# The next stage's input, normalised and transposed tile by tile during the running product

## The chip, the cores and the metric

The kernel runs on one core of a Trainium2 chip. The metric is the device time of one execution in microseconds. The core has TensorE (matmuls, transposes), VectorE, ScalarE, GpSimd and SyncE, which here issues the DMAs. In the profile they are called PE (PEld is its weight load), DVE, ACT, POOL and SP.

## The reference

It computes two transformer-like blocks on 512 tokens of width 1024, in float32. What matters here is the chain of stages at the end of the first block and the start of the second:

```python
x = x + gate1 * (merged @ w_o[l])                              # product 1: out_proj
h2 = rms_norm(x, norm2_w[l]) * (1.0 + scale2) + shift2
ff = jnp.square(jax.nn.relu(h2 @ w_mlp1[l])) @ w_mlp2[l]       # product 2: w_mlp2
x = x + gate2 * ff
...
h = rms_norm_2(x, norm_g)                                      # rglru_layer
u = h @ w_in
...                                                            # convolution, gates, linear scan
x = x + y @ w_out                                              # product 3: w_out_a
h = rms_norm_2(x_stream, norm_kv)                              # mla_shared_kv, mla_layer
ckr = h @ w_dkv
```

Each of the three marked products ends in x, whose rows are normalised (one root mean square per token) and are the input of the next product.

## The kernel before

*Tiles.* x lies in SBUF with tokens on the partitions: four token tiles t = 0 to 3 of 128 tokens, each in two halves b of 512 columns. A product that ends in x (`gemm_tm`) runs block b = 0 and then b = 1; a block needs all four token tiles and all its weights, 128 rows of the contraction per matmul. Every float32 operand is split into a high and a low part, so each step is three matmuls (`mm3`, L168 to L170): high with high, high with low, low with high. A weight piece (`weight`, L153 to L159) is loaded into wr, cast to wh by ScalarE, and the difference wl is made by VectorE or GpSimd; each of wr, wh and wl has four buffers.

*The end of a product.* In the last block (`touter`) the order is token tile by token tile: all steps of t = 0, then of t = 1, and so on. After the last matmul of a tile, `resid` multiplies by the gate (rt, L920) and adds to x (L921; L923 where there is no gate) on VectorE. `half_stats` takes the squares on ScalarE (sqj, L293) and, in the last block, the root r on GpSimd (L298, L299).

*The start of the next stage.* `transpose_norm` comes after the product in the code. For each token tile and each half kg it makes xn = x times r (L267, on GpSimd; in the third case on VectorE for kg = 1), four TensorE transposes into PSUM (pt, L271), where needed a scale and shift (nh, L280 on ScalarE, L283 and L286 on VectorE), and the split into high (ScalarE, L163) and low (VectorE, L164). So there are 8 transposes per token tile and 32 per hand-over. The new product then starts: `gemm_cm` with `halves=4` works four output blocks on token columns 0 to 255, then the same four on 256 to 511.

*The three hand-overs* are: first, out_proj to mlp (h2, called h in the profile); second, the last chunk of w_mlp2 to rglru (ha); third, w_out_a to mla_in (hb). w_out_a has five weight pieces per block, the others four.

*What sets the order.* The code issues instructions in its own order, and the tile framework's scheduler may move one ahead of another where nothing forbids it. What comes out is a fixed queue per engine, and each engine works through its queue in order. A tile in a pool has to wait for earlier tiles on the same memory. Pools belong to a `phase`, opened and closed like a stack on the left or right side of SBUF: in the kernel before, those of the next stage (the buffers of xn, h2 and nh) are opened after the running product's are closed, and so may lie over them.

Of the kernel before, what the change touches and what calls it, by code (L numbers as in the profile page):

```python
# [52 lines left out]
PAD = [0, 16, 56, 0, 32, 0, 32, 0, 0, 0, 56, 0, 48, 32, 0, 0, 0, 0, 0, 0]  # L53
# [6 lines left out]
class Build:  # L60
# [14 lines left out]
    def phase(self, nt=0, nbig=0, side="left", nw=0, nf=0, nx=0, nq=0):  # L75

        i = self.nm("p")
        with ExitStack() as st:
# [3 lines left out]
            p = {"sm": pool("sm", 2), "c": pool("c", 1)}  # L82
# [6 lines left out]
            if nbig:  # L89
                p["big"] = pool("big", nbig)  # L90
# [5 lines left out]
            if PAD[self.np]:  # L96
                self.nc.gpsimd.memset(p["c"].tile([128, PAD[self.np]], F32, name="pad" + i, tag="pad"), 0.0)
# [103 lines left out]
    def gemm_tm(self, blocks, lhs, evac, n, touter=False, gain=None, group=NT):  # L201


        for b, blk in enumerate(blocks):
# [4 lines left out]
            for ap in blk:  # L209
# [4 lines left out]
            order = [(t, i) for t in range(NT) for i in range(len(blk))] if hold else \  # L214
                [(t, i) for t0 in range(0, NT, group) for i in range(len(blk)) for t in range(t0, t0 + group)]
            for t, i in order:
                if i == 0 and t >= group:
# [6 lines left out]
                if i == len(blk) - 1:  # L224
                    evac(b, t, pss[t][:, :n])

# [33 lines left out]
    def transpose_norm(self, xt, rs, hi, lo, g=None, sh=None, key="xa"):  # L260

        nc = self.nc
        for t in range(NT):
            x = xt(t)
            for kg in range(2):
# [21 lines left out]
                self.split(hi[d], lo[d], h)  # L287

# [673 lines left out]
    def rglru(self):  # L962
# [10 lines left out]
        lam = self.load("lru_lambda", [128, 10])  # L973
        for b in (br, bi):
            nc.vector.tensor_scalar(out=b, in0=b, scalar1=0.5, scalar2=None, op0=ALU.mult)
        sp = self.c([128, 10], "sp")
        nc.vector.tensor_scalar(out=lam, in0=lam, scalar1=-1.0, scalar2=None, op0=ALU.mult)
        self.softplus(sp, lam, [self.small([128, 10], "spt", bufs=3) for _ in range(3)])
        spp = self.c([128, 10], "spp")
        spn = self.c([128, 10], "spn")  # L980
        nc.vector.tensor_scalar(out=spp, in0=sp, scalar1=4.0, scalar2=None, op0=ALU.mult)
        nc.vector.tensor_scalar(out=spn, in0=sp, scalar1=-4.0, scalar2=None, op0=ALU.mult)
# [4 lines left out]
        def xin(i, ps):  # L987
            xbs[i] = self.taps(ps, cw[:, i], cb[:, i:i + 1], [-3, -2, -1, 0])
# [7 lines left out]
        def product(jobs, halves=0):  # L996
            self.gemm_cm([[a["w_in_a"][i + 10 * (f is gin)]] for f, i in jobs], rhs,
                         lambda m, ps: jobs[m][0](jobs[m][1], ps), halves=halves)

        product([(xin, 0), (xin, 1), (gin, 0), (gin, 1)], halves=4)  # L1000
        for i0 in range(0, 10, 5):
# [32 lines left out]
            for j in range(5):  # L1034
# [3 lines left out]
                with self.fills():  # L1038
# [24 lines left out]
    def mla_in(self):  # L1063
# [13 lines left out]
        hh, hl = self.big("hb", F32R), self.big("hb", F32R)  # L1077
        self.transpose_norm(lambda t: xv[:, t], self.r4, hh, hl, key="xb")
# [4 lines left out]
                     lambda b, t, ps: nc.scalar.copy(out=ck[:, t], in_=ps), 320, gain=nkv)  # L1083
# [192 lines left out]
def emit(tc, a, out, dbg=None, stages=("b1", "b2")):  # L1276
    with ExitStack() as ctx:
        b = Build(tc, ctx, a, out, dbg)
        tail = ctx.enter_context(ExitStack())
# [181 lines left out]
```

## Time and profile before

| | |
|---|---|
| time, median of 3 runs | 1675.04 us (1671.86 to 1677.4) |
| time of the profiled execution | 1674.92 us |
| its span, first to last instruction | 1673.1 us |
| mean granted TensorE clock | 0.986 of full |
| TensorE busy | 1591.9 us, 95% |
| VectorE, ScalarE, GpSimd busy | 1130.0, 784.3, 447.4 us |
| chain that ended last | TensorE 40%, VectorE 4%, ScalarE 2%, GpSimd 2%, issue 1% |
| all 96 transposes of the hand-overs wait for xn | 29.5 us of weight-load and matmul waits |

The profile is of one execution. An engine's busy share is a mean over stages; a wait is put down to what ended it last. In a timeline row, equal instructions that follow each other are merged (x4), the first number is the start, the second the length from the first start to the last end, and a wait before it stands in brackets with its releaser. Matmuls overlap: the distance between starts is what each costs.

### The profile page before, as it was taken

What the parts mean: (1) busy time and instruction counts of PE and PEld (TensorE: products, weight loads), DVE (VectorE), ACT (ScalarE), POOL (GpSimd) and SP (SyncE); (2) the same over time, 40 slices, a digit from 0 to 9 for tenths busy, and PEclk for the clock granted to TensorE, in tenths of its full rate; (3) what the DMA queues carried; (4) which work ended last, traced back from release to release, by engine and by line L of the source; (5) the groups of instructions that cost most, each with busy time, mean ns of one, the idle gap of its engine ahead of it and who ended that gap; (6) DMA issues with size and microseconds to landing.
All of it is one profiled execution on the core that took longest, in us unless ns stands there. A gap on an engine that the chain in (4) does not pass through costs nothing. (4 is left out here: it accounts for less than half of the span.)

```text
span 1673.1 us, 20895 instructions
## 1 busy us (share of the span) xinstructions
PE 1591.9 (95%) x7696; PEld 1287.8 (77%) x7696; DVE 1130.0 (68%) x1948; ACT 784.3 (47%) x1511; POOL 447.4 (27%) x329
## 2 busy tenths in 40 slices
PE   5989999999999999999989999999989899999998
PEld 3767677677678778778879888888878777888886
DVE  7899689789869888973463343434457865757883
ACT  4357446354456666662353232323336562455552
POOL 3314345244353334321042020201131101521012
PEclk9999999999999999999999999999999999999999
DMA  7511223234223122225322233333313221322211
GB/s 257 187 53 62 63 76 127 63 101 134 78 63 101 57 83 88 87 74 177 93 76 88 89 101 100 91 99 101 101 52 114 78 79 52 100 78 67 67 64 51
DMA packets 50648, 153.54 MB, mean 92 GB/s; under 512 B 8177, under 2 KB 12913, under 8 KB 50546
## 3 DMA queue, kind: packets, MB, share of 16 engines
q1 hardware_dynamic: 50546, 152.22, 28.4%
q8 instruction: 60, 0.98, 0.2%
q14 instruction: 42, 0.34, 0.1%
HBM read 150.10 MB, written 2.10 MB: 91 GB/s over the span
## 5 line engine op out<-in xcount | busy, mean ns | idle before, releaser
L156 ACT CAST wh<-wr 128x1024 fp32r<-128x1024 f32 (+5 forms) x245 | 239.9, 980 | 417.7 <-PE pm L169 185.4
L159 DVE TENSOR_TENSOR wl<-wr,wh 128x1024 fp32r<-128x1024 f32 (+2 forms) x170 | 200.0, 1178 | 216.0 <-ACT wh L156 215.6
L159 POOL TENSOR_TENSOR wl<-wr,wh 128x1024 fp32r<-128x1024 f32 (+3 forms) x75 | 175.6, 2341 | 552.8 <-ACT wh L156 512.0
L168 PE MATMUL pm<-hh,wh 128*128 128x512 f32 x432 | 174.0, 407 | 8.5 <-ACT hh L163 6.8
L169 PE MATMUL pm<-hl,wh 128*128 128x512 f32 x432 | 175.5, 406 | 3.9 <-POOL hl L164 3.8
L170 PE MATMUL pm<-hh,wl 128*128 128x512 f32 x432 | 172.6, 400 | 0.0
L950 POOL TENSOR_TENSOR r<-r 128x512 f32<-128x512 f32 x32 | 50.8, 1589 | 260.1 <-ACT r L949 260.1
L168 PE MATMUL pm<-h,wh 128*128 128x512 f32 (+1 forms) x288 | 105.5, 368 | 0.0
L169 PE MATMUL pm<-h,wh 128*128 128x512 f32 (+1 forms) x288 | 105.4, 366 | 0.0
L170 PE MATMUL pm<-h,wl 128*128 128x512 f32 (+1 forms) x288 | 105.3, 366 | 0.0
L168 PEld LDWEIGHTS pm<-hh,wh 128*128 128x128 f32 x432 | 81.9, 190 | 30.2 <-ACT hh L163 8.3
L169 PEld LDWEIGHTS pm<-hl,wh 128*128 128x128 f32 x432 | 82.2, 190 | 26.9 <-POOL hl L164 7.2
L170 PE MATMUL pm<-wh,rl 128*128 128x512 f32 x256 | 99.6, 389 | 0.0
L168 PE MATMUL pm<-wh,rh 128*128 128x512 f32 x256 | 99.6, 389 | 0.0
L169 PE MATMUL pm<-wl,rh 128*128 128x512 f32 x256 | 99.6, 389 | 0.0
L731 POOL TENSOR_SCALAR pr<-pr,psum 128x512 f32<-128x512 f32 x64 | 64.6, 1021 | 128.8 <-DVE psum L727 70.7
L170 PEld LDWEIGHTS pm<-hh,wl 128*128 128x128 f32 x432 | 82.2, 190 | 19.7 <-issue 3.1
L478 DVE SCALAR_TENSOR_TENSOR acc<-pm,conv_w_s,acc 128x510 f32<-128x510 f32 (+2 forms) x118 | 87.7, 743 | 12.9 <-ACT acc L469 11.9
L614 POOL TENSOR_TENSOR e<-e,w 128x512 f32<-128x512 f32 x32 | 52.0, 1626 | 100.3 <-ACT e L613 85.9
L257 DVE SCALAR_TENSOR_TENSOR wada<-wada,cs 128x1024 f32<-128x1024 f32 x48 | 68.2, 1431 | 15.5 <-DMA wada<-in_w_ada 15.1
L726 ACT ACTIVATE pr<-px,nmax 128x512 f32<-128x512 f32 (+2 forms) x96 | 60.4, 637 | 29.9 <-DVE nmax L723 24.0
L168 PE MATMUL pm<-ha,wh 128*128 128x512 f32 (+1 forms) x192 | 69.0, 362 | 4.8 <-DVE acc L478 4.8
(401 smaller groups left out, 4138.3 us busy)
## 6 DMA issues: line engine op xcount, KB each, us to landing
wr<-in_w_mlp SPq DMA_DIRECT2D x64, 512.0 KB, 3.5
wada<-in_w_ada SPq DMA_DIRECT2D x48, 512.0 KB, 4.0
wr<-in_w_xbc SPq DMA_DIRECT2D x24, 512.0 KB, 3.5
wr<-in_w_in_a SPq DMA_DIRECT2D x20, 512.0 KB, 3.5
wr<-in_w_z SPq DMA_DIRECT2D x16, 512.0 KB, 3.6
wr<-in_w_ssd_out SPq DMA_DIRECT2D x16, 512.0 KB, 3.5
wr<-in_w_gate SPq DMA_DIRECT2D x16, 512.0 KB, 3.8
wr<-in_w_qkv SPq DMA_DIRECT2D x16, 384.0 KB, 3.0
```

The costliest lines, as they stand in the source:

```text
L156: nc.scalar.copy(out=hi[:, :n], in_=raw[:, :n])
L159: eng.tensor_tensor(out=lo[:, :n], in0=raw[:, :n], in1=r32(hi[:, :n]), op=ALU.subtract)
L168: m(out, lhsT=lh, rhs=rh, start=start, stop=False)
L169: m(out, lhsT=lh, rhs=rl, start=False, stop=False)
L170: m(out, lhsT=ll, rhs=rh, start=False, stop=stop)
L257: nc.vector.scalar_tensor_tensor(out=w, in0=w, scalar=1.0, in1=self.cs, op0=ALU.mult, op1=ALU.mult, accum_out=self.modc[:, j:j + 1])
L478: nc.vector.scalar_tensor_tensor(out=acc[:, lo:hi], in0=ps[:, lo + o:hi + o], scalar=w[:, j:j + 1], in1=acc[:, lo:hi], op0=ALU.mult, op1=A ...
L614: self.e("ew").tensor_tensor(out=e, in0=e, in1=w, op=ALU.mult)
L726: nc.scalar.activation(out=e[:, :n], in_=p, func=AF.Exp, bias=nmax, accum_out=s)
L731: self.e("norm").tensor_scalar(out=e[:, :n], in0=e[:, :n], scalar1=s, scalar2=1.0, op0=ALU.mult, op1=ALU.mult)
L950: self.e("sq").tensor_tensor(out=r, in0=r, in1=r, op=ALU.mult)
```

## The change

The new stage's norm is cut into a function per token tile (`token_norm`), and its pools are opened before the running product, on the other side of SBUF or in place of closed ones. `gemm_tm` gets `pre`: before token tile t of the last block it norms, transposes and splits tile t - 2 (`trail`), and after the last tile, tile 2. Tile 3 is done inside the next product: in `gemm_cm` after three of the four blocks on the first half of the tokens (`mid`), in `gemm_tm` of w_dkv before the last weight (`late`), whose token tile 3 comes last of all. In the last block of w_out_a the first two of five weights now pass over all token tiles first. The constants of rglru are loaded later, norm_kv and norm_b earlier. Pads are allocated without a memset.

```diff
-            p = {"sm": pool("sm", 2), "c": pool("c", 1)}
+            p = {}
+            if bare:
+                p["big"] = pool("big", nbig)
+            if not bare:
+                p["sm"] = pool("sm", 2)
+            if bare is not True:
+                p["c"] = pool("c", 1)
...
-                self.nc.gpsimd.memset(p["c"].tile([128, PAD[self.np]], F32, name="pad" + i, tag="pad"), 0.0)
+                p["c"].tile([128, PAD[self.np]], F32, name="pad" + i, tag="pad")
...
-    def gemm_cm(self, blocks, rhs, evac, halves=0, kouter=0, gain=None):
+    def gemm_cm(self, blocks, rhs, evac, halves=0, kouter=0, gain=None, mid=None):
...
+                        if mid and m == 0 and c0 == 0 and i == n - 2:
+                            mid()
...
-    def gemm_tm(self, blocks, lhs, evac, n, touter=False, gain=None, group=NT):
+    def gemm_tm(self, blocks, lhs, evac, n, touter=False, gain=None, group=NT, pre=None,
+                late=None):
...
-            order = [(t, i) for t in range(NT) for i in range(len(blk))] if hold else \
+            early = len(blk) - 3 if len(blk) > NW[1] else 0
+            order = [(t, i) for i in range(early) for t in range(NT)] + \
+                [(t, i) for t in range(NT) for i in range(early, len(blk))] if hold else \
                 [(t, i) for t0 in range(0, NT, group) for i in range(len(blk)) for t in range(t0, t0 + group)]
+            if late:
+                order = [(t, i) for i in range(len(blk)) for t in range(NT - 1)] + [(NT - 1, i) for i in range(len(blk))]
             for t, i in order:
+                if late and (t, i) == (0, len(blk) - 1):
+                    late()
+                if hold and pre and i == early:
+                    pre(t)
...
+            if hold and pre:
+                pre(NT)
...
-    def transpose_norm(self, xt, rs, hi, lo, g=None, sh=None, key="xa"):
+    def token_norm(self, rs, hi, lo, g=None, sh=None, key="xa"):
         nc = self.nc
-        for t in range(NT):
-            x = xt(t)
+        def run(t):
+            x = self.xv[:, t]
...
+        return run
+    def trail(self, norm):
+        return lambda t: norm(t - 2) if t >= 2 else None
...
-        a, mh, ml = self.a, self.mh, self.ml
+        nc, a, mh, ml = self.nc, self.a, self.mh, self.ml
         self.r2 = self.stats("r2")
-        self.gemm_tm([[a["w_o"][b, i] for i in range(4)] for b in range(2)], lambda k: (mh[:, k], ml[:, k]),
-                     lambda b, t, ps: self.resid(self.gb[16], b, t, ps, self.r2), 512, touter=True)
-        self.dump("x1", self.xv)
-    def mlp(self):
-        nc, a, xv = self.nc, self.a, self.xv
-        self.r3 = self.stats("r3")
         g2 = self.c([128, 8], "g2")
         nc.vector.scalar_tensor_tensor(out=g2, in0=self.modc[:, 32:40], scalar=1.0, in1=self.n2,
                                        op0=ALU.add, op1=ALU.mult)
-        hh, hl = self.big("h2", F32R), self.big("h2", F32R)
-        self.transpose_norm(lambda t: xv[:, t], self.r2, hh, hl, g2, self.modc[:, 24:32], key="xm")
+        self.h2 = self.big("h2", F32R), self.big("h2", F32R)
+        self.norm2 = self.token_norm(self.r2, *self.h2, g2, self.modc[:, 24:32], key="xm")
+        self.gemm_tm([[a["w_o"][b, i] for i in range(4)] for b in range(2)], lambda k: (mh[:, k], ml[:, k]),
+                     lambda b, t, ps: self.resid(self.gb[16], b, t, ps, self.r2), 512, touter=True,
+                     pre=self.trail(self.norm2))
+        self.dump("x1", self.xv)
+    def mlp(self, done):
+        nc, a, xv = self.nc, self.a, self.xv
+        self.r3 = self.stats("r3")
+        hh, hl = self.h2
...
-                         halves=4 if ch == 0 else 0)
+                         halves=4 if ch == 0 else 0, mid=lambda: self.norm2(3))
+            if ch == 3:
+                done()
+                na = self.load("norm_a", [128, 8])
+                self.ha = self.big("ha", F32R), self.big("ha", F32R)
+                self.norm3 = self.token_norm(self.r3, *self.ha, na, key="xa")
             self.gemm_tm([[a["w_mlp2"][ch, b, i] for i in range(4)] for b in range(2)], lambda k: rt[k],
                          lambda b, t, ps: self.resid(self.gb[40], b, t, ps, self.r3 if ch == 3 else None), 512,
-                         touter=ch == 3)
+                         touter=ch == 3, pre=self.trail(self.norm3) if ch == 3 else None)
...
-        na = self.load("norm_a", [128, 8])
-        hh, hl = self.big("ha", F32R), self.big("ha", F32R)
-        self.transpose_norm(lambda t: xv[:, t], self.r3, hh, hl, na, key="xa")
-        cw = self.load("conv_w_2", [128, 10, 4])
-        cb = self.load("conv_b_2", [128, 10])
-        br = self.load("b_rg", [128, 10])
-        bi = self.load("b_ig", [128, 10])
...
+        hh, hl = self.ha
+        K = {}
+        def consts():
+            self.norm3(3)
+            ready()
+            K["cw"] = self.load("conv_w_2", [128, 10, 4])
+            K["cb"] = self.load("conv_b_2", [128, 10])
+            K["br"] = self.load("b_rg", [128, 10])
+            K["bi"] = self.load("b_ig", [128, 10])
...
+            for n, f in (("spp", 4.0), ("spn", -4.0)):
+                K[n] = self.c([128, 10], n)
+                nc.vector.tensor_scalar(out=K[n], in0=sp, scalar1=f, scalar2=None, op0=ALU.mult)
...
-        def product(jobs, halves=0):
+        def product(jobs, halves=0, mid=None):
             self.gemm_cm([[a["w_in_a"][i + 10 * (f is gin)]] for f, i in jobs], rhs,
-                         lambda m, ps: jobs[m][0](jobs[m][1], ps), halves=halves)
-        product([(xin, 0), (xin, 1), (gin, 0), (gin, 1)], halves=4)
+                         lambda m, ps: jobs[m][0](jobs[m][1], ps), halves=halves, mid=mid)
+        product([(xin, 0), (xin, 1), (gin, 0), (gin, 1)], halves=4, mid=consts)
...
+        self.hb = self.big("hb", F32R), self.big("hb", F32R)
+        self.norm4 = self.token_norm(self.r4, *self.hb, key="xb")
         self.gemm_tm([[a["w_out_a"][b, i] for i in range(5)] for b in range(2)], lambda k: yT[k],
-                     lambda b, t, ps: self.resid(None, b, t, ps, self.r4), 512, touter=True)
+                     lambda b, t, ps: self.resid(None, b, t, ps, self.r4), 512, touter=True,
+                     pre=self.trail(self.norm4))
...
-        nkv = self.load("norm_kv", [128, 8])
-        nb = self.load("norm_b", [128, 8])
+        nkv, nb = self.nkv, self.nb
...
-        hh, hl = self.big("hb", F32R), self.big("hb", F32R)
-        self.transpose_norm(lambda t: xv[:, t], self.r4, hh, hl, key="xb")
+        hh, hl = self.hb
...
         self.gemm_tm([[a["w_dkv"][i] for i in range(4)]], lambda k: (hh[:, k], hl[:, k]),
-                     lambda b, t, ps: nc.scalar.copy(out=ck[:, t], in_=ps), 320, gain=nkv)
+                     lambda b, t, ps: nc.scalar.copy(out=ck[:, t], in_=ps), 320, gain=nkv,
+                     late=lambda: self.norm4(NT - 1))
...
-                inner.enter_context(b.phase(nf=NF2))
-                with b.phase(nt=NMLP, nbig=2):
-                    b.lo_pool = LO["mlp"]
-                    b.mlp()
...
+                O.close()
+                F.close()
+                b.mod_cols(16, 32)
+                b.gate_rows(16, 0.5)
+                b.gate_rows(40, 1.0)
+                M = stack(b.phase(nt=NMLP, side="right"), tail)
+                H = stack(b.phase(nbig=2, side="right", bare=True), tail)
+                b.out_proj()
+            inner.enter_context(b.phase(nf=NF2))
+            b.stack.insert(1, b.stack.pop())
+            B = ExitStack()
+            def place():
+                H.close()
+                B.enter_context(b.phase(nbig=2, bare="c"))
+                b.nkv, b.nb = b.load("norm_kv", [128, 8]), b.load("norm_b", [128, 8])
+            def ready():
+                M.close()
                 G.close()
+                R.enter_context(b.phase(nt=NRG))
```

In TensorE's queue before, at the first hand-over, these rows stand from out_proj's last matmuls to mlp's first:

```order
L169 MATMUL pm_7616<-wl_7637,mh_6867 128x512
L170 MATMUL pm_7616<-wh_7636,ml_6868 128x512
L271 MATMUL pt_7806<-ident,xn_7804 128x128 x4
L271 MATMUL pt_7820<-ident,xn_7818 128x128 x4
L271 MATMUL pt_7832<-ident,xn_7830 128x128 x4
L271 MATMUL pt_7846<-ident,xn_7844 128x128 x4
L271 MATMUL pt_7858<-ident,xn_7856 128x128 x4
L271 MATMUL pt_7872<-ident,xn_7870 128x128 x4
L271 MATMUL pt_7884<-ident,xn_7882 128x128 x4
L271 MATMUL pt_7898<-ident,xn_7896 128x128 x4
L168 MATMUL pm_7908<-h_7802,wh_7913 128x256
L168 MATMUL pm_7909<-h_7802,wh_7919 128x256
```

In the queue now, this is the place between out_proj's token tiles 1 and 2 (pm is the tile's accumulator, mh and ml the product's input):

```order
L175 MATMUL pm_7630<-wl_7653,mh_6860 128x512
L176 MATMUL pm_7630<-wh_7652,ml_6861 128x512
L294 MATMUL pt_7721<-ident,xn_7719 128x128 x4
L294 MATMUL pt_7735<-ident,xn_7733 128x128 x4
L174 MATMUL pm_7631<-wh_7634,mh_6860 128x512
L175 MATMUL pm_7631<-wl_7635,mh_6860 128x512
L176 MATMUL pm_7631<-wh_7634,ml_6861 128x512
```

Of the eight groups of four transposes two stand here, two before tile 3, two after the product, and two after the third block of mlp's first half.

On VectorE at the second hand-over, before: rt and x are the running product's gate and add, wl the next product's weights, nh the scale after the transposes.

```order
L920 TENSOR_TENSOR rt_10236<-pm_10184,gb_6866 128x512
L921 TENSOR_TENSOR x_6851<-x_6851,rt_10236 128x512
L920 TENSOR_TENSOR rt_10267<-pm_10185,gb_6866 128x512
L921 TENSOR_TENSOR x_6851<-x_6851,rt_10267 128x512
L920 TENSOR_TENSOR rt_10298<-pm_10186,gb_6866 128x512
L921 TENSOR_TENSOR x_6851<-x_6851,rt_10298 128x512
L159 TENSOR_TENSOR wl_10501<-wr_10499,wh_10500 128x1024
L159 TENSOR_TENSOR wl_10507<-wr_10505,wh_10506 128x1024
L920 TENSOR_TENSOR rt_10329<-pm_10187,gb_6866 128x512
L921 TENSOR_TENSOR x_6851<-x_6851,rt_10329 128x512
L159 TENSOR_TENSOR wl_10519<-wr_10517,wh_10518 128x1024
L283 TENSOR_TENSOR nh_10377<-pt_10372,norm_a_s 128x512
```

Now, from the same place, the end of token tile 0:

```order
L949 TENSOR_TENSOR rt_10244<-pm_10192,gb_6859 128x512
L950 TENSOR_TENSOR x_6847<-x_6847,rt_10244 128x512
L949 TENSOR_TENSOR rt_10275<-pm_10193,gb_6859 128x512
L306 TENSOR_TENSOR nh_10289<-pt_10284,norm_a_s 128x512
L950 TENSOR_TENSOR x_6847<-x_6847,rt_10275 128x512
L306 TENSOR_TENSOR nh_10300<-pt_10295,norm_a_s 128x512
L170 TENSOR_TENSOR ha_10043<-nh_10289,ha_10042 128x4x128
L170 TENSOR_TENSOR ha_10043<-nh_10300,ha_10042 128x4x128
L949 TENSOR_TENSOR rt_10328<-pm_10194,gb_6859 128x512
L306 TENSOR_TENSOR nh_10342<-pt_10337,norm_a_s 128x512
L950 TENSOR_TENSOR x_6847<-x_6847,rt_10328 128x512
L306 TENSOR_TENSOR nh_10353<-pt_10348,norm_a_s 128x512
```

The scale nh of one tile and the splits ha now stand between the adds of the tiles, and the first nh of a tile comes ahead of the next tile's x.

## Rows read from the trace of the kernel before

**Rows 1.** The page, busy us, share of the span and instructions by engine
```profile
PE 1591.9 (95%) x7696; PEld 1287.8 (77%) x7696; DVE 1130.0 (68%) x1948; ACT 784.3 (47%) x1511; POOL 447.4 (27%) x329
```

**Rows 2.** Windows: us, busy us (instructions) of five engines, PEclk, DMA share, GB/s
```profile
860.00:880.00 20.00, 14.29 (x81) 12.40 (x80) 16.71 (x22) 15.03 (x32) 12.12 (x13) 0.83 0.32 107
880.00:900.00 20.00, 20.00 (x165) 19.82 (x164) 4.81 (x5) 5.67 (x8) 3.60 (x3) 1.00 0.16 53
1220.00:1240.00 20.00, 14.57 (x85) 12.64 (x84) 17.41 (x23) 10.32 (x16) 10.55 (x10) 0.91 0.34 106
1420.00:1440.00 20.00, 16.62 (x84) 13.90 (x83) 14.91 (x21) 10.55 (x20) 12.21 (x14) 0.92 0.30 96
```

**Rows 3.** Timeline of PE, first hand-over: start, us, engine, line, op, out<-in, count
```profile
862.88 0.39 PE L170 MATMUL pm<-wh,ml 128*128 128x512 f32 x1
874.99 1.20 PE L168 MATMUL pm<-h,wh 128*128 128x256 f32 x4
876.84 0.36 PE L170 MATMUL pm<-h,wl 128*128 128x256 f32 x1
877.04 0.28 PE L168 MATMUL pm<-h,wh 128*128 128x256 f32 x1
```

**Rows 4.** Timeline of PE, second hand-over
```profile
1225.18 0.39 PE L170 MATMUL pm<-wh,rl 128*128 128x512 f32 x1
1225.41 1.47 PE L271 MATMUL pt<-ident,xn 128*128 128x128 f32 x12
1234.69 0.72 PE L168 MATMUL pm<-ha,wh 128*128 128x256 f32 x4
1238.75 0.32 PE L170 MATMUL pm<-ha,wl 128*128 128x256 f32 x1
1238.91 0.28 PE L168 MATMUL pm<-ha,wh 128*128 128x256 f32 x1
1239.03 0.28 PE L169 MATMUL pm<-ha,wh 128*128 128x256 f32 x1
```

**Rows 5.** Timeline of PE, third hand-over
```profile
1429.28 0.39 PE L170 MATMUL pm<-wh,yl 128*128 128x512 f32 x1
1429.51 1.03 PE L271 MATMUL pt<-ident,xn 128*128 128x128 f32 x8
1432.23 0.39 PE L168 MATMUL pm<-wh,hb 128*128 128x320 f32 x1
1440.14 0.35 PE L170 MATMUL pm<-wh,hb 128*128 128x320 f32 x1
1440.33 0.31 PE L168 MATMUL pm<-wh,hb 128*128 128x320 f32 x1
1440.48 0.31 PE L169 MATMUL pm<-wl,hb 128*128 128x320 f32 x1
```

**Rows 6.** Timelines of DVE and POOL, product 2, the chain of token tile 0
```profile
1209.29 0.69 DVE L920 TENSOR_TENSOR rt<-pm,gb 128x512 f32<-128x512 f32 x1 [2.41 <-PE pm L170]
1210.02 0.69 DVE L921 TENSOR_TENSOR x<-x,rt 128x512 f32<-128x512 f32 x1
...
1212.70 1.36 POOL L267 TENSOR_SCALAR xn<-x,r 128x512 f32<-128x512 f32 x2
```

**Rows 7.** Timeline of POOL, first hand-over; then xn by tile (ns min/median/max)
```profile
863.14 7.16 POOL L267 TENSOR_SCALAR xn<-x,r 128x512 f32<-128x512 f32 x6 [0.84 <-DVE wl L159]
871.27 2.89 POOL L267 TENSOR_SCALAR xn<-x,r 128x512 f32<-128x512 f32 x2
...
L267 POOL TENSOR_SCALAR xn<-x,r x20: 686/694/2272, 863.1 to 1436.1; 128x512 f32<-128x512 f32 x20
```

**Rows 8.** Timelines of DVE and POOL, second hand-over, where the two overlap
```profile
1226.34 1.96 DVE L921 TENSOR_TENSOR x<-x,rt 128x512 f32<-128x512 f32 x1
...
1225.39 2.36 POOL L159 TENSOR_TENSOR wl<-wr,wh 128x1024 fp32r<-128x1024 f32 x1 [0.78 <-ACT wh L156]
```

**Rows 9.** Timeline of SP in product 2: DMA issues
```profile
1181.86 0.80 SPq L1010 DMA_DIRECT2D wg<-in_w_gates  x2
```

More of the change, by code (lines that the diff above doesn't have):

```diff
@@ L52 @@
 FB = [32, 0]
-PAD = [0, 16, 56, 0, 32, 0, 32, 0, 0, 0, 56, 0, 48, 32, 0, 0, 0, 0, 0, 0]
+PAD = [0, 16, 56, 0, 32, 0, 32, 0, 0, 24, 0, 0, 40, 56, 32, 16, 0]
 def r32(ap):
@@ L74, in phase @@
     @contextmanager
-    def phase(self, nt=0, nbig=0, side="left", nw=0, nf=0, nx=0, nq=0):
+    def phase(self, nt=0, nbig=0, side="left", nw=0, nf=0, nx=0, nq=0, bare=False):
         i = self.nm("p")
@@ L88, in phase @@
                 p["q"] = pool("q", nq)
-            if nbig:
+            if nbig and not bare:
                 p["big"] = pool("big", nbig)
@@ L965, in rglru @@
         self.r4 = self.stats("r4")
-        na = self.load("norm_a", [128, 8])
-        hh, hl = self.big("ha", F32R), self.big("ha", F32R)
-        self.transpose_norm(lambda t: xv[:, t], self.r3, hh, hl, na, key="xa")
-        cw = self.load("conv_w_2", [128, 10, 4])
-        cb = self.load("conv_b_2", [128, 10])
-        br = self.load("b_rg", [128, 10])
-        bi = self.load("b_ig", [128, 10])
[L973 to L982, printed above, removed]
+        hh, hl = self.ha
[7 more added lines that the diff above has]
+            K["bi"] = self.load("b_ig", [128, 10])
+            lam = self.load("lru_lambda", [128, 10])
+            for b in (K["br"], K["bi"]):
+                nc.vector.tensor_scalar(out=b, in0=b, scalar1=0.5, scalar2=None, op0=ALU.mult)
+            sp = self.c([128, 10], "sp")
+            nc.vector.tensor_scalar(out=lam, in0=lam, scalar1=-1.0, scalar2=None, op0=ALU.mult)
+            self.softplus(sp, lam, [self.small([128, 10], "spt", bufs=3) for _ in range(3)])
+            for n, f in (("spp", 4.0), ("spn", -4.0)):
+                K[n] = self.c([128, 10], n)
+                nc.vector.tensor_scalar(out=K[n], in0=sp, scalar1=f, scalar2=None, op0=ALU.mult)
         rhs = lambda k: (hh[:, k], hl[:, k])
@@ L987, in xin @@
         def xin(i, ps):
-            xbs[i] = self.taps(ps, cw[:, i], cb[:, i:i + 1], [-3, -2, -1, 0])
+            xbs[i] = self.taps(ps, K["cw"][:, i], K["cb"][:, i:i + 1], [-3, -2, -1, 0])
         def gin(i, ps):
@@ L1273, in mla, with emit, stack @@
                      touter=True)
-def emit(tc, a, out, dbg=None, stages=("b1", "b2")):
+def emit(tc, a, out, dbg=None):
     with ExitStack() as ctx:
         b = Build(tc, ctx, a, out, dbg)
-        tail = ctx.enter_context(ExitStack())
+        def stack(phase=None, at=ctx):
+            x = at.enter_context(ExitStack())
+            if phase is not None:
+                x.enter_context(phase)
+            return x
+        tail = stack()
         with b.phase(nw=NW), ExitStack() as inner:
@@ L1336, in emit @@
-            if "b2" in stages:
-                with b.phase(nt=NRG):
-                    with b.phase(nbig=2):
-                        b.lo_pool = LO["rglru"]
-                        b.rglru()
-                tail.enter_context(b.phase(nq=8, side="right"))
-                with b.phase(nbig=2, nt=NMI):
-                    b.lo_pool = LO["mla_in"]
-                    b.mla_in()
-                with b.phase(nt=NMLA):
-                    b.lo_pool = LO["mla"]
-                    b.mla()
+            b.mod_setup()
@@ new lines, in emit @@
+            with ExitStack() as A:
+                A.enter_context(b.phase(nbig=3))
+                b.cs = b.c([128, 1024], "cs")
+                cpool = b.pool("c")
+                big = lambda n, p=b.pool("big"): p.tile([128, 8, 512], F32R, tag="big", name=b.nm(n))
+                b.hh, b.hl, b.accS = b.big("hh", F32R), b.big("hl", F32R), b.big("accS")
+                with b.phase(nt=9, nbig=1, nx=2 * NX):
+                    b.lo_pool = LO["start"]
+                    b.silu_c()
+                    first = b.norm1()
+                    b.cpool = cpool
+                    b.ssd_setup()
+                    b.cpool = None
+                F = stack(b.phase(nf=NF), A)
+                with b.phase(nt=NSSD):
+                    b.lo_pool = LO["ssd"]
+                    b.ssd(first)
+                O = stack(b.phase(nbig=2), A)
+                b.oh, b.ol = b.big("oh", F32R), b.big("ol", F32R)
+                with b.phase(nt=NATT):
+                    b.lo_pool = LO["attn"]
+                    b.attention()
+                tail.enter_context(b.phase(nbig=1, side="right"))
+                b.lo_pool = LO["merge"]
+                b.residual_setup()
+                G = stack(b.phase(side="right"), tail)
+                b.gb = {j: b.c([128, 1024], f"gb{j}") for j in (16, 40)}
+                b.mh, b.ml = big("mh"), big("ml")
+                with b.fills():
+                    b.merge()
+                O.close()
[6 more added lines that the diff above has]
+                b.out_proj()
@@ new lines, in emit @@
+            inner.enter_context(b.phase(nf=NF2))
[7 more added lines that the diff above has]
+                M.close()
+                G.close()
+                R.enter_context(b.phase(nt=NRG))
+            b.lo_pool = LO["mlp"]
+            b.mlp(place)
@@ L1350, in pack @@
+            with ExitStack() as R:
+                b.lo_pool = LO["rglru"]
+                b.rglru(ready)
+            tail.enter_context(b.phase(nq=8, side="right"))
+            with b.phase(nt=NMI):
+                b.lo_pool = LO["mla_in"]
+                b.mla_in()
+            B.close()
+            with b.phase(nt=NMLA):
+                b.lo_pool = LO["mla"]
+                b.mla()
 def pack(i):
```

52 lines of the change are left out of this document (2 added, 50 removed).

## The prediction

> **What bounds the kernel now.** I first read the busy line of the page: TensorE 1591.9 of 1673.1 us, 95%, the others far below [rows 1]. So the time is TensorE's work plus its holes, 81 us in all. Next the table of 20 us windows, to find the holes: TensorE is busy 20.00 of 20 in a window inside a product (880 to 900), but 14.29, 14.57 and 16.62 in the three windows in which one product hands over to the next, and there the granted clock is 0.83, 0.91 and 0.92 instead of 1.00 [rows 2]: part of the time TensorE runs at 1.2 instead of 2.4 GHz. Last TensorE's timeline in each hand-over, to price them.
>
> I price a hand-over as the time from the end of the old product's last matmul to the first matmul of the new one that has its full-clock spacing, less the work in it at full clock. Spacings: 0.23 us for a 512-wide matmul (1225.18 to 1225.41), 0.12 for a 256-wide one (1238.91 to 1239.03), 0.15 for a 320-wide one (1440.33 to 1440.48), and 0.11 for a transpose (12 in a row take 1.47 us, 8 take 1.03; the difference over 4) [rows 4, 5].
> - First: ends at 862.88 + 0.23 = 863.11, full spacing from 877.04: 13.9 us. In it 32 transposes (3.5) and 9 matmuls from 874.99 to 876.84 (1.1). Lost: 9.3 us [rows 3].
> - Second: 1225.41 to 1238.91, 13.5 us. In it 32 transposes (3.5) and 18 matmuls, 1234.69 to 1238.75 (2.2). Lost: 7.8 us [rows 4].
> - Third: 1429.51 to 1440.33, 10.8 us. In it 28 transposes (3.1) and 15 matmuls, 1432.23 to 1440.14 (2.2). Lost: 5.5 us [rows 5].
>
> Sum 22.6 us: the most that the change can take back, idle and slow clock together.
>
> Why the holes are there: all 32 transposes stand in TensorE's queue behind the old product's last matmul. In the first hand-over even the vector work waits: GpSimd's first xn starts at 863.14, right after that matmul [rows 3, 7], because its pool lies over memory that the product reads. In the second xn of the first token tile is ready at 1214.06, 11 us before the product ends [rows 6], and only the place of the transposes in the queue makes it late.
>
> **Part by part.** *Transposes and matmuls.* The same 96 transposes and the same matmuls are issued, so nothing is added. Two token tiles (16 transposes) stand inside the old product, one at its end, one inside the next product. None sits behind a hole if its xn is ready when TensorE comes to it.
>
> *Is xn ready?* The chain from a tile's last matmul to its second xn (gate multiply, add, squares, root, two xn) takes 4.77 us where nothing disturbs it: 1209.29 to 1212.70 + 1.36 [rows 6]. What TensorE has meanwhile is one tile, 24 x 0.23 = 5.5 us, and from the second turned tile on 8 transposes more, 0.9: 6.4. So the first turned tile of a hand-over never waits. For the next ones the chain grows. In the second hand-over the vector queue now puts one 128x512 multiply of the tile before ahead of the add; at the add's 0.69 the chain is 5.5 [rows 6]. The vector work of the tile before also slows xn: alone 0.69, beside vector work 7.16/6 = 1.19 in the first hand-over, 2.27 at worst [rows 7]. With 1.19 the chain is 6.5 against 6.4: a stall of 0.1 for tile 1. Tile 2 also meets the new weights' casts on ScalarE and differences on VectorE or GpSimd; one such piece took 2.36 us [rows 8], and I take 1 us of stall for it in the second hand-over. In the first the multiply comes behind the add: I take 0.2 for both tiles. Bounds: 0 and, at 2.27 per xn, 8.6 - 6.4 = 2.2 us per tile.
>
> *Third hand-over.* The fixed order gives each tile 18 matmuls, 4.1 us, plus 0.9. The chain has no gate multiply: 4.77 - 0.73 (the step from 1209.29 to 1210.02) = 4.0, or 4.5 with one slowed xn (the other is VectorE's). I take 0.1. The order by tile needs the fifth weight only after two weights' passes over all tiles, 2 x 24 x 0.23 = 11 us into the block, so the four buffers hold.
>
> *The last tile.* Its chain runs beside the next product, which first has three blocks of token columns 0 to 255: 0.9 + 3 x 24 x 0.12 = 9.5 us. Before, this chain ended at 871.27 + 2.89 = 874.16, 11.0 us after the product [rows 7], but behind six slow xn that are now gone. Between 0 and 1.5 us I take 0.5. In the third product the cover is 0.9 + 54 x 0.15 = 9.0 us for a chain of 4 to 5: nothing.
>
> *Weights after the third hand-over.* Its new order uses the last tile for all four weights at the end, 24 x 0.15 = 3.6 us, so a weight buffer of the next product comes free only 2.7 us before that product. Cast and difference of a 768-wide piece: the cast has no row here (between 0.7 and 2 by the 512-wide pieces; I take 1), the difference on GpSimd 768/1024 x 2.36 = 1.8 [rows 8], with the hand-offs 3.1. I take 0.4 us, bounds 0 and 1.5. Before, this was covered.
>
> *Loads.* Five small constant loads go into SyncE's queue ahead of one weight load, at 0.40 us each 2 us [rows 9]. Their wait is for the same product that the gate weights waited for in that row, at 1181.86. The weight behind them serves a block that starts four tiles before 1225.41, at 1203: 20 us of cover, so nothing. The vector operations on these constants move too, but stay inside the running product. The dropped memsets of the pads were off the path.
>
> Sum: 22.6 recovered, less 0.2 + 1.1 (second) + 0.1 + 0.5 + 0.4 = 2.3 of new stalls: 20.3 us. The profiled execution took 1674.92 us (its span 1673.1 and 1.8 around it), as good as the median 1675.04. 1674.9 - 20.3 = 1654.6 us; its own range, with all stalls at zero (1652.3) or about twice to three times as large (1659), is 1652 to 1659.
>
> **A rule that speaks against it.** GpSimd and VectorE hinder each other here: an add of 0.69 us took 1.96 while GpSimd worked on a weight difference from 1225.39 to 1227.75 [rows 6, 8]. The Trainium skill ("SBUF — State Buffer", Who interferes with whom) says that a VectorE instruction with two SBUF inputs and a GpSimd instruction that reads SBUF share one port, and that the later one waits for the other to finish. That row agrees. By the rule each xn beside the new vector work would wait for a whole vector instruction instead of growing by the mean; what that gives is the first rival, which is priced from rows alone.
>
> **Rivals.**
> 1. *xn loses to VectorE each time.* Two splits, two multiplies and the new tile's add now fall into the time in which xn runs. At 2.27 per xn, tiles 1 and 2 of the first two hand-overs stall 2.2 us each (8.8), and in the third, with one xn on GpSimd, 4.0 + 1.6 - 5.0 = 0.6 twice. Recovered: 22.6 - 8.8 - 1.2 - 0.9 (last tile, weights) = 11.7, so 1663. For it: 2.27 is in the trace. Against: the median of the 20 is 0.694 [rows 7], and xn needs only come in time, not fast.
> 2. *The wait moves into the product and repeats: slower.* In the second hand-over the multiply that waits for the transposes stands ahead of the next tile's add, and the transposes wait for the xn that follows from the add. A late tile so makes the next one late. If every tile's chain is like the last one of the first hand-over, 11.0 us, the nine inner places stall 11.0 - 5.5 once and 11.0 - 6.4 twice in the first two (29 us), and 11.0 - 4.1 once and 11.0 - 5.0 twice in the third (19): 48 us against 22.6, 1700 us. It decides the sign from a mean stall of 22.6/9 = 2.5 us per place, a chain of about 8.5. Against: 4.77 was measured beside the running product, and TensorE has its clock after short waits.
> 3. *The change does not bring it.* The next stage's matmuls start earlier but then wait for weights, whose casts and differences compete with the norm's vector work, so that the hole only moves. At under 5 us left: 1670 to 1675. For it: ScalarE and VectorE are busy 15 and 17 of 20 us in the first window. Against: in the following window, 880 to 900, TensorE is full and VectorE needs 4.81 of 20 [rows 2], so there is room to catch up.
>
> **Chances and range.** Forecast 0.69, rival 1 0.17, rival 2 0.05, rival 3 0.09. The measurement tells 0.3%, 5 us, from no change: below 1670.0 is faster. Faster 0.69 + 0.17 = 0.86, same 0.09, slower 0.05. The range goes from 1650, the bound 1652.3 less the 2 us by which runs spread, to 1667, beyond rival 1. That leaves out rivals 2 and 3.
>
> **What would show it.** In the timeline of TensorE: 8 transposes ahead of token tiles 2 and 3 of each product's last block, each with no idle or under 1 us before them; no gap over 1 us between the old product's last matmul and the new one's first besides 8 transposes; full clock in all three windows, and busy time near 20 of 20. xn of the first tile in the first hand-over starting some 12 us before the product's end. Each hand-over shorter by 9, 7 and 5 us, and nothing else moved by more than 1 us. I am wrong if waits on xn inside a product sum to more than 5 us, if the clock still falls in these windows, or if the stage behind a hand-over shows new waits for wh or wl.

## The result, and the profile after

The changed kernel takes 1655.39 us (median of 4 runs, 1653.86 to 1657.45), the kernel before 1674.38 beside it: ratio 0.9889, interval 0.9875 to 0.9903. The forecast was 1654.6. The profiled execution took 1655.45 us, its span 1653.7, against 1674.92 and 1673.1 before: 19.4 us less span.

The busy line of the page after, against [rows 1]:

```profile
PE 1583.5 (96%) x7696; PEld 1280.6 (77%) x7696; DVE 1130.0 (68%) x1948; ACT 783.9 (47%) x1511; POOL 445.6 (27%) x322
```

The windows that were short before (columns as in [rows 2]; the last two are the second and third hand-over):

```profile
860.00:880.00 20.00, 18.69 (x136) 17.42 (x135) 14.01 (x18) 12.13 (x25) 9.78 (x8) 1.00 0.33 106
880.00:900.00 20.00, 20.00 (x140) 18.73 (x140) 8.97 (x10) 9.84 (x15) 6.33 (x4) 1.00 0.32 96
1220.00:1240.00 20.00, 19.06 (x157) 18.57 (x156) 11.44 (x14) 6.65 (x10) 8.45 (x7) 1.00 0.33 106
1420.00:1440.00 20.00, 19.91 (x131) 19.61 (x130) 14.52 (x38) 10.10 (x25) 5.83 (x5) 1.00 0.38 117
```

TensorE is busy 18.69, 19.06 and 19.91 of 20 us instead of 14.29, 14.57 and 16.62, with the clock at 1.00 in all of them. What is left are waits on xn. In the timeline of TensorE after, first hand-over, then the place in the second and the one in the third that wait:

```profile
853.70 1.04 PE L294 MATMUL pt<-ident,xn 128*128 128x128 f32 x8
860.03 1.03 PE L294 MATMUL pt<-ident,xn 128*128 128x128 f32 x8
866.37 0.60 PE L294 MATMUL pt<-ident,xn 128*128 128x128 f32 x4
868.27 0.66 PE L294 MATMUL pt<-ident,xn 128*128 128x128 f32 x4 [1.31 <-POOL xn L290]
877.40 1.03 PE L294 MATMUL pt<-ident,xn 128*128 128x128 f32 x8
...
1222.42 0.66 PE L294 MATMUL pt<-ident,xn 128*128 128x128 f32 x4 [0.94 <-POOL xn L290]
...
1406.91 1.09 PE L294 MATMUL pt<-ident,xn 128*128 128x128 f32 x8 [0.30 <-POOL xn L290]
```

Eight transposes stand ahead of tiles 2 and 3, eight between the products and eight inside the next one. Those inside the product wait for nothing in the first two hand-overs and 0.30 us in the third; the larger waits, 1.31 and 0.94 us, are at tile 2, between the products. GpSimd and VectorE at the first of these (start, us, engine, line):

```profile
851.88 1.36 POOL L290 TENSOR_SCALAR xn<-x,r 128x512 f32<-128x512 f32 x2
857.52 2.09 POOL L290 TENSOR_SCALAR xn<-x,r 128x512 f32<-128x512 f32 x2
863.84 4.38 POOL L290 TENSOR_SCALAR xn<-x,r 128x512 f32<-128x512 f32 x2
```

```profile
863.76 1.23 DVE L165 TENSOR_TENSOR wl<-wr,wh 128x1024 fp32r<-128x1024 f32 x1 [0.78 <-ACT wh L162]
864.90 1.71 DVE L170 TENSOR_TENSOR h<-nh,h 128x512 fp32r<-128x512 f32 x2
866.53 1.21 DVE L165 TENSOR_TENSOR wl<-wr,wh 128x1024 fp32r<-128x1024 f32 x1
```

One xn takes 0.68 us for tile 0, 1.05 for tile 1 and 2.19 for tile 2, where VectorE makes weight differences (wl) and splits (h) without a pause. That is rival 1's mechanism, at one tile of three.

Four stretches, each from the first matmul of one product to that of another, show where the 19.4 us came from (worked out from the starts in TensorE's timelines; us):

| stretch | before | after | less | forecast |
|---|---|---|---|---|
| start to out_proj | 819.5 | 820.9 | -1.5 | 0 |
| out_proj to w_mlp2 (first hand-over) | 101.3 | 93.5 | 7.8 | 9.3 - 0.2 - 0.5 = 8.6 |
| w_mlp2 to w_out_a (second) | 449.2 | 442.3 | 7.0 | 7.8 - 1.1 = 6.7 |
| w_out_a to the end (third) | 303.1 | 297.0 | 6.1 | 5.5 - 0.1 - 0.4 = 5.0 |

The first line holds nothing of the change: over the runs below it lies between 817.0 and 821.4.

### The profile page after: what moved, and what is told of

Read it like the earlier page. It is cut to its first block, busy times and chain, and to the rows that moved or that the text cites. A ratio compares the mean times of both kernels' runs of the same rounds, so it can differ in the third digit from the quotient of the medians.

```text
span 1653.7 us, 20877 instructions
## 1 busy us (share of the span) xinstructions
PE 1583.5 (96%) x7696; PEld 1280.6 (77%) x7696; DVE 1130.0 (68%) x1948; ACT 783.9 (47%) x1511; POOL 445.6 (27%) x322
## 4 chain that ended last, share of the span: by engine, by line
PE 67%; DVE 17%; ACT 4%; issue 3%; POOL 3%; DMA 1%; SPq 0%; DVEq 0%; POOLq 0%; ACTq 0%
PE pm L175 18%; PE pm L174 18%; PE pm L176 18%; DVE acc L507 2%; DVE nmax L752 1%; PE px L608 1%; PE px L848 1%; DVE w L635 1%; DVE wl L165 1%; DMA wada<-in_w_ada 1%; PE px L598 1%; POOL rs L254 1%; DVE wada L279 1%; PE px L857 1%; POOL wl L165 1%
```

## Experiments

All times are medians, the ratios to the kernel before on the same chip (1673.6 to 1674.0 us there). "Place" is the place of a hand-over's transposes in TensorE's queue.

**1. All three hand-overs back, new pools kept.**

```diff
-                     ..., 512, touter=True, pre=self.trail(self.norm2))
+                     ..., 512, touter=True)
+        for t in range(NT):
+            self.norm2(t)
...
-                         halves=4 if ch == 0 else 0, mid=lambda: self.norm2(3))
+                         halves=4 if ch == 0 else 0)
```

and likewise for norm3 and norm4 (there `late` goes too). The changed order of the weights in w_out_a, the moved loads and the dropped memsets stay.

> The pools of the changed kernel, with the transposes of all three hand-overs put back behind the product as they stood before. Theory (the place in TensorE's queue brings the gain, the pools only make the place possible): the token tiles still follow the product's last matmul one chain later, so nearly all is lost again, 1669 to 1675 us, with TensorE waiting 6 to 9 us ahead of the transposes at each hand-over; a part of the first hand-over's 9.3 may stay won, since its three xn buffers no longer wait for the product's own. Rival (the pools alone bring it, because xn and the h halves no longer share buffers with the running product): 1655 to 1661 us and no wait over 2 us at the transposes.

Measured 1668.14 us (1663.48 to 1669.37), ratio 0.9963, 0.9949 to 0.9977. So 12.8 of some 19 us are lost, not all. By stretches: the first hand-over 98.2 us (3.1 better than before, 4.7 worse than after), the second 449.2 (as before), the third 297.2 (as after!). Windows of this run, the three hand-overs:

```profile
860.00:880.00 20.00, 16.15 (x116) 14.66 (x115) 14.73 (x21) 12.32 (x28) 7.05 (x7) 0.91 0.33 106
1220.00:1240.00 20.00, 15.15 (x106) 14.19 (x105) 13.00 (x19) 6.61 (x11) 9.16 (x8) 0.83 0.29 98
1420.00:1440.00 20.00, 19.45 (x133) 18.23 (x132) 13.02 (x19) 10.11 (x18) 8.43 (x9) 1.00 0.36 116
```

The time is 0.9 us under the theory's range, and the waits on xn at the transposes are 3.8, 4.8 and 0 us by hand-over, not 6 to 9. The theory holds for the second hand-over and for part of the first; in the third, 19.45 of 20 without any change of place was in neither expectation. The profiled execution is the fastest of the six, 1663.48 us, 4.7 under their median (its stretch before out_proj is 817.0, the shortest of all), so its stretches can make the first hand-over look better than it mostly is.

**2. Only the first hand-over in the new place** (norm3 and norm4 put back as in experiment 1, norm2 not).

> Only the first hand-over keeps its new place; the second and the third are put back behind their products, all in the new pools. Theory (three separate gains that add up): the second hand-over loses 6.9 us again and the third 5.1, so 1655.4 + 12.0 = 1667.4 us, 1666 to 1669. Rival (the gains hang together, since whoever is late at one hand-over is late at the next one's weights too, or the first one is most of the gain): under 1663 us, or over 1671 us.

Measured 1661.19 us (1660.91 to 1661.61), ratio 0.9926, 0.9911 to 0.9941: not the additive figure, and under the 1663 that the rival named. That the gains hang together isn't shown, though: the stretches are 93.5, 447.0 and 297.2, so the first hand-over is as in the changed kernel, the second loses 4.7 of its 7.0, and the third loses nothing. The time is 7.0 below experiment 1, the first hand-over's place, and only 5.8 above the changed kernel, where 12.0 was expected for two. The third's share is missing again.

**3. The third hand-over taken apart: place and order of the weights.** The change has a second edit there, which the prediction counted as harmless: the last block of w_out_a has five weights and four buffers. Before, the queue held 24 matmuls of each token tile, and the fifth weight's six for tiles 0 to 2 came near the block's end; these tiles were finished 26, 21 and 16 matmuls (6.0, 4.8 and 3.7 us) before it. Now two weights pass over all tiles first, and it is 54, 36 and 18 matmuls (12.4, 8.3 and 4.1 us). Four kernels on one chip: the changed one, place undone, order undone (below), both undone.

```diff
-            early = len(blk) - 3 if len(blk) > NW[1] else 0
+            early = 0
```

> The changed kernel once more, as the base for the three kernels run beside it: 1654 to 1657 us. Theory on the clock (the short fall of the granted clock near the start of w_out_a's product, seen before and in the run with one tile's distance, is chance and not tied to the change): it may show in this profile or not, and is worth 1 to 2 us where it does. Rival (the change removes it): it is absent here again.

> The changed kernel with the third hand-over's transposes alone put back behind the product (and w_dkv's order as before); the order of w_out_a's last block, two weights over all tiles first and then tile by tile, stays. The prediction's step (the place in TensorE's queue gives this hand-over its gain): 5.1 us lost again, about 1660.5. New theory (here the order of the weights gives the gain, since tiles 0 to 2 are finished 12, 8 and 4 us before the product's end, so that their transposes find xn ready behind the product): 0 to 1.5 us lost, 1655 to 1657.

> The changed kernel with the old order of w_out_a's last block (tile by tile over all five weights; with four buffers the fifth weight's matmuls of tiles 0 to 2 fall to the end), the transposes in their new place. New theory (the order finishes the tiles in time): tiles 0 to 2 are finished 30, 25 and 20 matmuls before the end, all within 7 us, so the transposes still wait 3 to 6 us together, some of it inside the product: 1658 to 1662 us. The prediction's step (the place does it): under 1.5 us lost, 1655 to 1657.

> Third hand-over as in the kernel before in both respects, old order of the weights and transposes behind the product, in the new pools; the first two hand-overs as changed. Both theories: the third hand-over's 5.5 us (its hole in the kernel before) are lost again, 1659.5 to 1662.5 us, since what is left of the change there is its pools. Rival (the pools give it): 1655 to 1657.

| us, median (range) | new order | old order |
|---|---|---|
| new place | 1655.14 (1654.50 to 1658.08) | 1658.95 (1654.31 to 1661.87) |
| old place | 1655.86 (1654.51 to 1657.39) | 1658.24 (1657.13 to 1658.76) |

The place is worth 0.7 us with the new order, within the spread, and nothing with the old; the order 2.4 to 3.8, though the ranges overlap a little. The third stretch of the four profiles, which leaves out the chance of all that comes before, says the same: 298.3 and 298.7 us with the new order (new place, old place), 302.7 and 301.3 with the old. TensorE at the third hand-over with old place and new order, then with both old, then with new place and old order:

```profile
1416.30 2.19 PE L294 MATMUL pt<-ident,xn 128*128 128x128 f32 x16
1419.25 0.63 PE L294 MATMUL pt<-ident,xn 128*128 128x128 f32 x4 [0.48 <-POOL r L327]
```

```profile
1414.18 1.04 PE L294 MATMUL pt<-ident,xn 128*128 128x128 f32 x8
1416.05 1.09 PE L294 MATMUL pt<-ident,xn 128*128 128x128 f32 x8 [0.83 <-POOL xn L290]
1419.66 0.66 PE L294 MATMUL pt<-ident,xn 128*128 128x128 f32 x4 [2.23 <-POOL xn L290]
```

```profile
1415.76 1.09 PE L294 MATMUL pt<-ident,xn 128*128 128x128 f32 x8 [1.92 <-POOL xn L290]
1417.42 0.71 PE L294 MATMUL pt<-ident,xn 128*128 128x128 f32 x4 [0.57 <-POOL xn L290]
1420.92 0.79 PE L294 MATMUL pt<-ident,xn 128*128 128x128 f32 x4
```

With the tiles finished in time, 16 transposes behind the product run without a wait. With the tiles finished late they wait wherever they stand: 0.83 and 2.23 us behind the product (0.83 and 2.53 in the kernel before), 1.92 and 0.57 inside it. But "inside" is not far inside there: with the old order the first transposes stand 15 matmuls ahead of the product's end, where the changed kernel has them 36 and 18 ahead. That place was not tried with the old order. Both undone lost 3.1 us, under the 5.5 that both theories gave. The waits are nearly the ones of before, but the clock stayed at 1.00 here, where it was 0.92 before [rows 2]; with the new place and the old order it fell again. The windows of both undone, then of new place and old order:

```profile
1400.00:1420.00 20.00, 16.94 (x84) 13.63 (x83) 10.55 (x15) 8.70 (x17) 10.86 (x13) 1.00 0.19 58
```

```profile
1400.00:1420.00 20.00, 17.52 (x78) 13.83 (x77) 7.34 (x11) 6.07 (x12) 7.04 (x10) 0.95 0.13 37
1420.00:1440.00 20.00, 19.90 (x130) 18.85 (x129) 14.47 (x36) 9.62 (x21) 7.77 (x6) 0.97 0.22 67
```

Why it fell there and not here is open; by the windows it is worth some (0.05 + 0.03) x 20 = 1.6 us of the 302.7.

**4. One tile's distance instead of two.**

```diff
-        return lambda t: norm(t - 2) if t >= 2 else None
+        return lambda t: norm(t - 1) if t >= 1 else None
```

with `mid` and `late` dropped.

> Each token tile is normalised and turned one tile after it is made instead of two; the transposes stand 14 to 18 matmuls into the next tile in the first and second product and 11 in the third (24, 24 and 18 plus the tile between in the changed kernel, counted from the tile's end). Theory (the distance must cover the chain of about 4.8 us): 14 matmuls of 0.24 us cover 3.3 us, 18 cover 4.3 and 11 cover 2.6, so each place waits 0.5 to 2.2 us, nine places together 10 to 16 us: 1665 to 1671 us, with waits of that size on xn at each place. Rival (the chain is shorter when nothing crowds it, 3 us or so): under 1.0 us at each place, 1655 to 1659 us.

Measured 1676.09 us (1669.05 to 1681.10), ratio 1.0010, 0.9994 to 1.0026: all of the gain is gone. TensorE's wait for xn in the list of waits (us in sum, times, longest), this run and the changed kernel:

```profile
PE pt L294 <- POOL xn L290: 17.3, 12, 2.4
```

```profile
PE pt L294 <- POOL xn L290: 2.5, 3, 1.3
```

The size of each wait (0.87 to 2.37 us) is close to what was expected, the time 5 us above the range: I summed nine places and there are twelve (the last tile of each hand-over waits too), and I left the clock out. It falls to 0.91 in the window of the second hand-over and in the one that begins as the third's last transposes do, 2 x 0.09 x 20 = 3.6 us:

```profile
1220.00:1240.00 20.00, 16.48 (x96) 14.35 (x95) 12.39 (x17) 7.95 (x13) 8.37 (x9) 0.91 0.31 106
1440.00:1460.00 20.00, 19.90 (x120) 19.74 (x121) 11.94 (x34) 8.22 (x21) 4.44 (x3) 0.91 0.28 89
```

**5. Half of each xn on VectorE, first two hand-overs.**

```diff
-        "xm0": "gpsimd", "xm1": "gpsimd", "xa0": "gpsimd", "xa1": "gpsimd",
+        "xm0": "gpsimd", "xm1": "vector", "xa0": "gpsimd", "xa1": "vector",
```

> As the changed kernel, but the second half of each xn of the first and second hand-over (xm1, xa1) is made by VectorE and not by GpSimd, as the third hand-over has it. Theory (the waits of 1.31 and 0.94 us that are left come from GpSimd's two xn after each other, 2.19 us each beside VectorE's copies): both shrink to about 0.3 us, 1653.0 to 1654.8 us, ratio to the changed kernel 0.9985 to 0.9997. Rival (VectorE is itself in the way there: 0.7 us more of it per tile puts the residual of the next tile off): no gain or up to 2 us slower, 1655 to 1658 us.

> The kernel with the second half of each xn of the first two hand-overs on VectorE once more, beside the next kernel. Theory (the two waits that it removes are worth 2.25 us): 1652 to 1653.5 us, about 2.5 below the changed kernel's 1655.1 and 1655.4. Rival (the first reading of 1652.3 was low by the spread between calls): 1653.5 to 1655.5.

Measured 1652.32 us (ratio 0.9870, 0.9853 to 0.9887) and 1652.11 (0.9876, 0.9861 to 0.9891). The waits of 1.31 and 0.94 are gone; what is left of waits on xn in the first of the two profiles is 0.34 and 0.33. The two xn after each other on GpSimd were what these places waited for. The first time lies 0.7 us under its expected range, the second in its range; they are 2.8 to 3.3 us below the changed kernel's 1655.14 and 1655.39 for 2.25 of waits. By stretches the first hand-over shows 1.5 of it (92.0 in both profiles, 93.5 in both of the changed kernel); the second shows no clear gain (441.8 and 443.0 against 442.3 and 442.8).

**6. All xn on VectorE** (`xb0` as well).

> As the changed kernel, but all 24 xn are made by VectorE (0.49 us each where it makes them, against 0.69 to 2.2 on GpSimd). Theory (xn on GpSimd was slow because it runs beside VectorE's two-input instructions; off GpSimd nothing collides): each xn 0.49 us, waits on xn of 0.3 us at most at each place, 1651 to 1652.5 us. Rival (VectorE's own queue is now the longer way: 1 us of xn per tile ahead of casts' differences and of the residual): waits of 0.5 to 1.5 us at the third tiles come back, 1653.5 to 1657.

Measured 1651.37 us (1650.66 to 1658.31), ratio 0.9877, 0.9858 to 0.9896. Its median is the lowest of all; against experiment 5 the 0.8 us are within the spread. xn by tile, and the place that waited 1.31 us after:

```profile
L290 DVE TENSOR_SCALAR xn<-x,r x24: 475/484/489, 850.1 to 1416.3; 128x512 f32<-128x512 f32 x24
```

```profile
864.70 1.04 PE L294 MATMUL pt<-ident,xn 128*128 128x128 f32 x8
```

Each xn takes 0.48 us, and no transpose waits for it at any of the twelve places.

**7. One tile's distance and half of each xn on VectorE.**

> One tile's distance as in the run before with it, but with the second half of each xn of the first two hand-overs on VectorE, which shortens the chain by 0.4 to 0.9 us and moves no matmul. Theory (the wait at a place is the chain less the distance, one for one, and the clock falls with the long ones): the eight waits there, 10.1 us together, shrink to 3 to 7, and the time from 1676.1 to 1667 to 1672 us. Rival (the chain's end is not what those waits wait for, or VectorE is delayed by as much): waits within 1 us of 10.1 in sum, 1674 to 1678.

Measured 1679.82 us (1678.72 to 1683.12), ratio 1.0040, 1.0026 to 1.0054: slower, which neither expectation had. The waits at tile 1 of the first hand-over, experiment 4 and here, each with GpSimd's xn that it waits for:

```profile
858.37 1.32 PE L294 MATMUL pt<-ident,xn 128*128 128x128 f32 x8 [0.87 <-POOL xn L290]
857.62 1.36 POOL L290 TENSOR_SCALAR xn<-x,r 128x512 f32<-128x512 f32 x2
```

```profile
859.73 1.09 PE L294 MATMUL pt<-ident,xn 128*128 128x128 f32 x8 [1.38 <-POOL xn L290]
858.69 0.98 POOL L290 TENSOR_SCALAR xn<-x,r 128x512 f32<-128x512 f32 x1
```

The four transposes of the second half stand behind those of the first, so the second xn was nearly covered already; the wait is for the first. That one became slower, 0.98 instead of 0.68 us, beside VectorE's other half made at the same time. These 0.30 are most of the 0.51 by which the wait grew; the rest stood behind the first four transposes before, where the row is 1.32 us long and not 1.09. At tile 2 the loss is larger: one xn takes 2.03 us where two took 1.95, and the wait is 2.59 instead of 1.83.

```profile
866.11 1.95 POOL L290 TENSOR_SCALAR xn<-x,r 128x512 f32<-128x512 f32 x2
```

```profile
867.23 2.03 POOL L290 TENSOR_SCALAR xn<-x,r 128x512 f32<-128x512 f32 x1
869.32 1.97 PE L294 MATMUL pt<-ident,xn 128*128 128x128 f32 x8 [2.59 <-POOL xn L290]
```

The eight waits of the first two hand-overs sum to 13.5 us instead of 10.1. Shortening the chain helps only at its end that is waited for.

## Why the prediction came out

- **The total was right:** 1654.6 against 1655.39, and the 22.6 us of loss were the right pool to draw from. That it came so close is partly luck, as the third hand-over shows.
- **"Only the place of the transposes in the queue makes it late": right for the second hand-over.** 7.0 us recovered against 6.7; without the place 0 (experiment 1, 449.2) or 2.2 (experiment 2, 447.0) is, and 5.3 us lie between the medians without it (experiment 2) and with it (experiment 3, old place of the third alone).
- **For the first it is the larger part of the cause.** 7.8 of the 8.6 forecast came. By the stretches 4.7 of them are the place and 3.1 come without it; by the medians of experiments 1 and 2 the place is 7.0, which leaves 0.8. What comes without it goes with the pools: three xn buffers are then free before the product's end, and GpSimd's first xn starts at 847.98 in experiment 1, 12.5 us before that product's last matmul, where before it waited for it [rows 7]. The prediction saw this wait and gave it no share. No run undoes the pools alone. The three xn of experiment 1 that are made before the product's end:

```profile
847.98 1.36 POOL L290 TENSOR_SCALAR xn<-x,r 128x512 f32<-128x512 f32 x2
853.34 0.70 POOL L290 TENSOR_SCALAR xn<-x,r 128x512 f32<-128x512 f32 x1
```

- **For the third it failed.** The step that put its 5.5 us down to the place is wrong. The order of w_out_a's weights brings 2.4 to 3.8 us and the place, once the order is there, under 1. The prediction dismissed this edit with "the four buffers hold"; it read only that the new order costs nothing, not that the old one finished tiles 0 to 2 within 6 us of the end. The forecast came out by luck, since place and order were changed together.
- **The stalls, 2.3 us, were right in sum and wrong in place.** Tile 2 of the second was 0.94 (forecast 1.1). The first had 1.31 (0.2), more than the 1 us that was allowed between two products; last tiles 0 (0.5), the third's tile 0 0.30 (0.1), the weights behind the third hand-over 0.09 at most by that window's 19.91 of 20 (0.4).
- **Rival 1** happened at tile 2 alone, where 2.19 per xn is its 2.27; at tile 0 and 1 VectorE had pauses. Two xn took 4.38 us beside two-input instructions of VectorE and 1.36 at tile 0. The Trainium skill ("SBUF — State Buffer", Who interferes with whom) says that such instructions and GpSimd's reads lock each other out; the trace agrees. It also says that some one-input forms can contend; 0.98 instead of 0.68 us in experiment 7 agrees with that.
- **Rival 2** did not happen at a distance of two tiles, but its threshold was too high: I had the sign turn at a mean wait of 2.5 us; experiment 4 has 17.3 / 12 = 1.44 and no gain left, since twelve places wait and not nine, and the clock, which I took to hold after short waits, fell in two windows. Its mechanism shows there in the first hand-over: behind the vector work of the tile before, the gate multiply rt of tiles 1 to 3 starts 0.86, 1.32 and 1.38 us after the start of the tile's last matmul, where 0.43 is usual. In the second hand-over it is 0.43 at all four tiles. Tile 2 of the first, with the splits h of tile 1 ahead of it:

```profile
861.25 1.29 DVE L170 TENSOR_TENSOR h<-nh,h 128x512 fp32r<-128x512 f32 x2
862.46 0.68 DVE L949 TENSOR_TENSOR rt<-pm,gb 128x512 f32<-128x512 f32 x1
```

- **Rival 3** is refuted: 19.0 us came, and the window behind the first hand-over is full, 20.00 of 20.

About 1.3 us of the profiled difference in the third stretch (297.0 after, 298.3 in the second profile of the changed kernel) is not the change's. In the first block of w_out_a's product, some 25 us in, the clock was 0.91 before and 1.00 after; the changed kernel run again has 0.91 there (first row: before, second: after, third: again). It is 0.91 there in 7 of the 13 profiles:

```profile
1380.00:1400.00 20.00, 18.11 (x68) 13.29 (x67) 18.33 (x22) 6.66 (x10) 3.34 (x2) 0.91 0.26 90
```

```profile
1380.00:1400.00 20.00, 18.54 (x80) 14.78 (x80) 11.29 (x14) 6.57 (x13) 1.81 (x5) 1.00 0.35 119
```

```profile
1380.00:1400.00 20.00, 19.23 (x79) 15.54 (x78) 10.46 (x13) 5.52 (x11) 2.11 (x5) 0.91 0.34 118
```

## What to carry over

A hole between two products had two causes here, and they needed different cures: the consumer's transposes stood too late in the queue (second hand-over, and most of the first), or the producer's tiles were all finished too late (third); the timeline of the old product's last block, tile by tile, tells which. Where two edits go together, price each as if the other weren't there. And before a chain is shortened, see which of its pieces the consumer's first instruction waits for.

## Not expected of the hardware

- TensorE stayed at full clock through waits of 1.31 us, and of 0.83 and 2.23 in experiment 3 (both undone, window at 1.00), but not through 1.92 and 0.57 there (old order alone, 0.95 and 0.97). In experiment 4 it fell to 0.91 in the window with waits of 1.81 and 1.69 and in the one behind the wait of 2.37, and did not in two others with waits of 1.83. No run here separates these.
- GpSimd's xn beside one of VectorE's with a single SBUF input takes 0.98 us instead of 0.68. VectorE's own stays at 0.49 where it starts first, as all twelve in experiment 7 do by 0.06 us or so; in experiment 5 one that started 0.55 us after GpSimd's took 0.92:

```profile
873.64 0.92 DVE L290 TENSOR_SCALAR xn<-x,r 128x512 f32<-128x512 f32 x1
873.09 1.19 POOL L290 TENSOR_SCALAR xn<-x,r 128x512 f32<-128x512 f32 x1
```
